# The first layer's first RMS norm takes the route of the other norms, and a subtraction for the rank-64 decay and rate weights changes engine and place

## Chip, core and metric

The kernel runs on one core of one Trainium2 chip. The metric is the device time of a launch in microseconds (us). The kernel before took 1690.54 us as the median of 3 runs (1690.29 to 1692.25).

## What is computed

A decoder trunk of two pre-norm residual layers over 512 positions of width 1024, in float32. What matters here is the head of each layer: an RMS norm, and one wide projection whose columns are then split among three token mixers and their gates.

```python
def rmsnorm(x, g):
    xf = x.astype(jnp.float32)
    y = xf * lax.rsqrt(jnp.mean(xf * xf, axis=-1, keepdims=True) + EPS) * g.astype(jnp.float32)
    return y.astype(x.dtype)
...
    for l in range(DEPTH):
        h = rmsnorm(x, norm1_g[l])
        p = h @ w_in[l]
        p_rw, p_ret, p_sg, gate_logits = jnp.split(p, in_cuts, axis=-1)
        y_rw = rwkv7_branch(p_rw, ...)
...
    # in rwkv7_branch, with wd, ad of rank 64 cut from p
    w = -jax.nn.softplus(-(w0 + jnp.tanh(wd) @ w_up)) - 0.5
    a = jax.nn.sigmoid(a0 + ad @ a_up)
```

## The kernel before, in words

**Layout and precision.** Activations lie with features on the 128 partitions and the 512 positions along the free axis, so that x is eight tiles of 128x512. Products are made to nearly full precision from pairs: each operand is split into a high part (a cast to the fp32r type, on ScalarE, ACT in the profile) and a low part (source minus high, on VectorE, DVE), and `mm3` issues three matmuls for each product (high weight with low x, high with high, low with high). All 128x512 matmuls at line 157 are these.

**The norm is applied late.** The matmuls run on g times x, without the root of the mean square. A finished column group (128 output features, 512 positions, one accumulator bank in PSUM, tile `acc`) is multiplied on its way out of PSUM by `rsF`, a 128x512 tile that holds 1/rms of each position on all partitions (`col`, line 525, output `rwp`). So the matmuls need not wait for the norm, but the first evacuation of an accumulator does. There are four accumulators (pool `pa`) and four smaller result banks (pool `ps`, tile `sm`). A fifth column can start only when one of the first four has been read.

**Layer 0's start.** `run` loads the eight x tiles and the first weight blocks by an order that is written out as a string of steps: z (scale and split of an x tile), s (its square, added up in `acc` of the norm's state, here called the sum of squares, tile `sq`), w (cast and subtraction of one weight block). `firstK` (line 306) then walks the contraction in eight blocks k = 0 to 7 of 128 features, each feeding all four accumulators (columns 12, 4, 0, 8 of the projection; 12 holds the decay and rate ranks): 12 matmuls for each k. Between k = 5 and k = 6 `norm_stats` (line 268) sums the squares over the partitions by four fp32 matmuls with one column (line 272), adds epsilon on VectorE (line 274) and takes the power -1/2 on GpSimd (POOL, line 276). Between k = 6 and k = 7 `norm_rows` (line 279) spreads the result over the partitions by four fp32 transposes (line 281), and ScalarE copies it to `rsF` (line 283).

**The other norms** use `norm_bcast` (line 285): the sum of squares is split into a pair, two fp32r matmuls with a matrix of ones sum and spread it in one go (lines 290 and 291, result `sm`), ScalarE takes the square root (line 293, tile `rms`; it needs another activation table than the one in use), VectorE takes four reciprocals of 128x128 into `rsF` (line 297). In layer 1's first norm a 32x32 block transpose on VectorE (line 300) and four GpSimd copies also make `rsT`, the same numbers with positions on the partitions.

**The rank-64 weights.** `rwkv` loads two 128x512 matrices `wua`, whose two halves of the partitions both hold the same 64 rows; ScalarE casts the whole to fp32r (`wus`, line 515), and GpSimd replaces the lower half by the remainder (line 519), so that one matmul sums both parts. They are used in `prep` (lines 565 and 566).

**Order and queues.** Each engine works through its own list in order. Where a call is wrapped in `keep_in_program_order`, its place among such calls is fixed; all else is placed by a list scheduler of the framework, which sets the order of each engine's list at build time. Weight blocks come by the SyncE DMA queue (SP) into three raw buffers (`wr`), are cast into one of three `wh` buffers and subtracted into one of three `wl` buffers; a load waits until its raw buffer has been cast and subtracted, and a cast waits until TensorE (PE) has used the `wh` buffer's last contents.

Of the kernel before, what the change touches and what calls it, by code (L numbers as in the profile page):

```python
# [16 lines left out]
D = 1024  # L17
S = 512
NC = 4
# [33 lines left out]
class Emit:  # L53
# [91 lines left out]
    def split(self, src, al=None):  # L145

        al = al or self.u
        hi, lo = al(dt=F32R, n="hi"), al(dt=F32R, n="lo")
        self.nc.scalar.copy(hi, src)
        self.nc.vector.tensor_tensor(lo, src, hi, op=SUB)  # L150
        return hi, lo

    def mm3(self, ps, w, x, start, stop, **kw):
# [111 lines left out]
    def norm_new(self):  # L265
        return {"z": [], "acc": None}

    def norm_stats(self, st):
        nc = self.nc
        pt = self.sm((128, 4))  # L270
        for c in range(NC):
            self.tc.keep_in_program_order(nc.tensor.matmul(pt[:, c:c + 1], st["acc"][:, c * 128:c * 128 + 128], self.c("ones")[:, 0:1], start=True, stop=True))
        ms = self.small((128, 4), "ms")
        nc.vector.tensor_scalar(ms, pt, 1.0 / D, 1e-6, op0=MUL, op1=ADD)
        self.rsT = self.small((128, 4), "rs")
        nc.gpsimd.tensor_tensor(self.rsT, ms, self.c("mhalf")[:, 0:4], op=POW)

    def norm_rows(self):
        pb = self.sm()
        for c in range(NC):  # L280
            self.tc.keep_in_program_order(self.nc.tensor.transpose(pb[:, c * 128:c * 128 + 128], self.rsT[:, c:c + 1].to_broadcast([128, 128]), self.c("ident")))
        self.rsF = self.small((128, 512), "rsF", bufs=1)
        self.nc.scalar.copy(self.rsF, pb)

    def norm_bcast(self, st, cols):

        nc, po = self.nc, self.tc.keep_in_program_order
        hi, lo = st["sq"]
        pb = self.sm()
        po(nc.tensor.matmul(pb, self.ones, lo, start=True, stop=False))  # L290
        po(nc.tensor.matmul(pb, self.ones, hi, start=False, stop=True))
        rms = self.u(n="rms")
        nc.scalar.activation(rms, pb, AF.Sqrt, scale=1.0 / D, bias=self.c("eps"))
        self.rsF = self.small((128, 512), "rsF", bufs=1)
        for c in range(NC):
            cs = slice(c * 128, c * 128 + 128)
            nc.vector.reciprocal(self.rsF[:, cs], rms[:, cs])
        if cols:
            t = self.u((128, 4, 4, 32), n="rst")
            nc.vector.transpose(t.rearrange("p c b r -> p (c b r)"), self.rsF)  # L300
            self.rsT = self.small((128, 4), "rs")
            for b in range(4):
                nc.gpsimd.tensor_copy(self.rsT[32 * b:32 * b + 32, :], t[32 * b:32 * b + 32, :, b, 0])

    def firstK(self, st):

        self.h, self.pin = st["z"], True
        pss = [self.acc() for _ in FIRST]
        for k in range(8):
            if k == 6:  # L310
                self.norm_stats(st)
            elif k == 7:
                self.norm_rows()
            hi, lo = self.unit("wk0", 0, k, 0)
            cs = [slice(i * 128, i * 128 + 128) for i in range(NC)]
            if k == 0:
                for w, x in ((hi, 0), (hi, 1), (lo, 0)):
                    for ps, s in zip(pss, cs):
                        self.tc.keep_in_program_order(self.nc.tensor.matmul(ps, w[:, s], self.h[0][x], start=w is hi and x == 0, stop=False))  # L319
                continue  # L320
            for ps, s in zip(pss, cs):
                self.mm3(ps, (hi[:, s], lo[:, s]), self.h[k], False, k == 7)
        self.pin = False
        return pss

    def firstF(self, l, ids, st, at):


        self.h = st["z"]
        pss = [self.acc() for _ in ids]  # L330
        gs = [self.matFg(ps, ("wall", l, i, 0), self.h) for ps, i in zip(pss, ids)]
        self.pin = True
        for i, g in enumerate(gs + gs):
            if i == at:
                self.norm_bcast(st, l and ids[0] == 12)
            next(g)
        self.pin = False
        return pss
# [10 lines left out]
    def run(self):  # L349
        nc, tc, a, V = self.nc, self.tc, self.a, self.nc.vector  # L350
        self.con = self.cp.tile([128, NCC], F32, name="con")
        self.pre, self.tsum = [], {}
        self.rst = self.cp.tile([128, 512], F32, name="rst")
        self.bonesR = self.cp.tile([128, 128], F32R, name="bonesR")
        self.ones = self.cp.tile([128, 128], F32R, name="ones")
        V.memset(self.rst, 1.0)
        wu = self.acc()
        for i in range(5):
            nc.tensor.matmul(wu[:, 0:256], self.rst[:, 0:128], self.rst[:, 256:512], start=True, stop=True)  # L359
        st = self.norm_new()  # L360
        first = tc.tile_pool(name="x0", bufs=1)
        x0 = first.__enter__().tile([128, 520], F32, name="x0g", tag="x0g")
        self.pc = x0[:, 512:520]
        xs = [x0[:, 0:512]] + [self.u(n="x") for _ in range(7)]
        self.keep = True
        with tc.high_priority():
            for j in range(8):
                q, o, i = (nc.scalar, xs[j], a["xT"][:, j, :]) if j in (1, 3) else (nc.sync, xs[j], a["xT"][:, j, :])
                tc.keep_in_program_order(q.dma_start(*((o, i) if j else (x0, a["x0g"]))))
                if self.plan and j in (0, 1, 2):  # L370
                    self.load(self.plan[self.nraw], nc.sync if j else nc.scalar)
        tc.keep_in_program_order(nc.scalar.copy(self.small((128, 1), "ms"), self.rst[:, 0:1]))
        tc.keep_in_program_order(nc.scalar.copy(self.ones, self.rst[:, 0:128]))
        for step in "z0 w z1 w z2 w z3 s0 s1 w z4 s2 z5 s3 w c z6 s4 w z7 s5 s6 s7 w w".split():
            if step == "w":
                if self.plan:
                    if self.nraw == self.npart:
                        self.load(self.plan[self.nraw])
                    self.part(self.plan[self.npart])
            elif step == "c":  # L380
                g1 = self.pc
                self.load_pc(0)
                tc.keep_in_program_order(nc.scalar.dma_start(self.con, a["con"]))
                self.pc, g1 = g1, self.pc
            elif step[0] == "z":
                self.norm_z(st, xs[int(step[1])], "n1")
            else:
                self.norm_sq(st, xs[int(step[1])])
        self.keep, self.pc = False, g1
        first.__exit__(None, None, None)  # L390
        xd = [a["xT"][:, j, :] for j in range(8)]
        for l in range(L):
            mg = self.mixer(l, st)
            st = self.norm_new()
            x = self.wout(l, mg, xd, st)
            st["sq"] = self.split(st["acc"])
            act = self.ffn_up(l, st, x if l == L - 1 else None)
            if l == L - 1:
                self.last(act)
            else:  # L400
                st = self.norm_new()
                x, xd = self.ffn_down(l, act, x, st)
                st["sq"] = self.split(st["acc"])
            self.rp.__exit__(None, None, None)
            self.fp = None
# [88 lines left out]
    def rwkv(self, l, nst):  # L494
# [16 lines left out]
        Ws = []  # L511
        for i in range(2):
            wua, s = self.u(n="wua"), self.u(dt=F32R, n="wus")
            self.tc.keep_in_program_order(nc.scalar.dma_start(wua, a["wua"][l, i]))
            A.copy(s, wua)
            Ws.append((wua, s))
        ready = dict(zip(FIRST, self.firstF(l, FIRST[:3], nst, 3) if l else self.firstK(nst)))
        for i, (wua, s) in enumerate(Ws):
            self.tc.keep_in_program_order(P.tensor_tensor(s[64:128, :], wua[64:128, :], s[64:128, :], op=SUB))
            Ws[i] = s  # L520

        def col(m):
            ps = ready.pop(m) if m in ready else self.colF(l, m)
            p = self.r(n="rwp")
            V.tensor_tensor(p, ps, self.rsF, op=MUL)  # L525
            t = self.r(n="rwc")
            A.activation(t, p, AF.Identity, scale=omu[:, m:m + 1])
            V.scalar_tensor_tensor(t[:, 1:], p[:, :511], self.p("mu", m), t[:, 1:], op0=MUL, op1=ADD)
            return t

        wa = col(12)
        Xs = []
        for i in range(2):
            x = self.u(n="wax")
# [947 lines left out]
```

## Time and profile before

| what | us |
|---|---|
| three runs, median | 1690.54 |
| three runs, lowest and highest | 1690.29 and 1692.25 |
| span of the profiled execution, first to last instruction | 1688.8 |
| TensorE busy in it | 1680.2 |
| VectorE busy | 1217.9 |
| ScalarE busy | 793.7 |
| GpSimd busy | 261.3 |

The profile gives one execution on the chip by its instructions; its own time is its span and the start and end around it, which no row shows. The median of the runs lies 1.74 us above the span, and this difference is taken for what lies around it. A row of the timeline gives start, duration, engine, line, operation, output<-inputs and, in brackets, how long the engine had been idle and what ended that. PE rows are matmuls, whose ends are modelled; the distance between the starts of two matmuls tells more than the duration of one. "x4" means that several instructions were merged in a row.

### The profile page before, as it was taken

To read this page: it belongs to the slowest core of one execution; us is meant where nothing else is said; L and a number is where in the kernel's file an instruction comes from. 1 tells how busy PE (TensorE), PEld (TensorE's weight loads), DVE (VectorE), ACT (ScalarE), POOL (GpSimd) and SP (SyncE) were. 2 spreads that over 40 slices of the span, in tenths; PEclk is the share of its full clock that TensorE was granted. 3 is DMA by queue.
4 is the path that set the end of the run, shared out by engine and by line. 5 is a ranking of instruction groups with operands and counts; after the bars stand their busy time and mean duration, and the time that the engine had idled before them with its cause. 6 is when DMAs were issued, how large, how long until landed. Compare 5 with 4: busy or idle time off the path is not lost.

```text
span 1688.8 us, 27952 instructions
## 1 busy us (share of the span) xinstructions
PE 1680.2 (99%) x10247; PEld 1381.5 (82%) x10247; DVE 1217.9 (72%) x2115; ACT 793.7 (47%) x1365; POOL 261.3 (15%) x376
## 2 busy tenths in 40 slices
PE   9999999999999999999999999999999999999998
PEld 7888877888888888888888888778888888888887
DVE  7887746578669877655568888465786688887877
ACT  6563433554255444433346544335542544444565
POOL 1121000312301200003321210003122012220000
PEclk9999999999999999999999999999999999999999
DMA  5236563634544533247743366536344434443775
GB/s 183 88 109 199 176 187 95 184 122 134 191 144 148 195 122 97 63 146 261 252 145 99 94 207 184 174 101 188 118 137 163 154 96 144 142 141 110 244 248 177
DMA packets 143385, 260.01 MB, mean 154 GB/s; under 512 B 19440, under 2 KB 35440, under 8 KB 143248
## 3 DMA queue, kind: packets, MB, share of 16 engines
q1 hardware_dynamic: 117056, 188.41, 35.9%
q0 software_dynamic: 17552, 54.15, 9.8%
q10 hardware_dynamic: 8640, 15.67, 2.6%
q8 instruction: 80, 1.31, 0.3%
q14 instruction: 57, 0.47, 0.1%
HBM read 212.94 MB, written 45.22 MB: 153 GB/s over the span
## 4 chain that ended last, share of the span: by engine, by line
PE 97%; DVE 1%; DMA 1%; issue 0%; ACT 0%; SPq 0%; ACTq 0%; DVEq 0%
PE acc L157 88%; PE sm L157 3%; PE sm L696 2%; PE sm L948 1%; PE sm L603 1%; PE sm L1059 0%; DMA wr<-wall 0%; DMA tr<-bkT 0%; DVE wl L141 0%; PE acc L359 0%; PE sm L566 0%; PE sm L565 0%; PE sm L1006 0%; PE sm L850 0%; PE acc L319 0%
## 5 line engine op out<-in xcount | busy, mean ns | idle before, releaser
L157 PE MATMUL acc<-lo,sh 128*128 128x512 f32 x1108 | 432.0, 390 | 0.0
L157 PE MATMUL acc<-hi,sh 128*128 128x512 f32 x1108 | 431.4, 389 | 0.0
L157 PE MATMUL acc<-hi,sl 128*128 128x512 f32 x1108 | 424.6, 389 | 0.0
L140 ACT CAST sh<-wr 128x512 fp32r<-128x512 f32 (+1 forms) x375 | 226.8, 614 | 309.1 <-PE acc L157 165.6
L141 DVE TENSOR_TENSOR sl<-wr,sh 128x512 fp32r<-128x512 f32 (+1 forms) x375 | 252.0, 680 | 94.9 <-ACT sh L140 78.9
L141 DVE TENSOR_TENSOR wl<-wr,wh 128x512 fp32r<-128x512 f32 x238 | 169.0, 713 | 139.4 <-ACT wh L140 133.6
L140 ACT CAST wh<-wr 128x512 fp32r<-128x512 f32 x238 | 146.8, 619 | 242.8 <-PE acc L157 154.6
L157 PEld LDWEIGHTS acc<-lo,sh 128*128 128x128 f32 x1108 | 208.0, 188 | 43.8 <-issue 0.3
L157 PEld LDWEIGHTS acc<-hi,sl 128*128 128x128 f32 x1108 | 208.0, 188 | 43.1 <-issue 0.2
L157 PEld LDWEIGHTS acc<-hi,sh 128*128 128x128 f32 x1108 | 208.0, 188 | 43.0
L157 PE MATMUL acc<-lo,wh 128*128 128x512 f32 x584 | 230.0, 394 | 0.4 <-DVE rwp L525 0.4
L157 PE MATMUL acc<-hi,wl 128*128 128x512 f32 x584 | 228.3, 391 | 0.1
L157 PE MATMUL acc<-hi,wh 128*128 128x512 f32 x584 | 227.6, 390 | 0.0
L1125 ACT ACTIVATE cv<-fu,pc 128x512 f32<-128x512 f32 x88 | 71.7, 816 | 138.4 <-DVE fu L1123 138.4
L157 PEld LDWEIGHTS acc<-hi,wl 128*128 128x128 f32 x584 | 109.6, 188 | 24.6 <-issue 0.9
L157 PEld LDWEIGHTS acc<-lo,wh 128*128 128x128 f32 x584 | 109.6, 188 | 24.2 <-DVE rwp L525 0.8
L157 PEld LDWEIGHTS acc<-hi,wh 128*128 128x128 f32 x584 | 109.7, 188 | 22.3 <-issue 0.2
L157 PE MATMUL acc<-ah,sh 128*128 128x512 f32 x352 | 108.4, 389 | 0.0
L1126 DVE SCALAR_TENSOR_TENSOR cv<-fu,pc,cv 128x511 f32<-128x511 f32 x88 | 65.8, 749 | 34.5 <-ACT cv L1125 34.4
L157 PE MATMUL acc<-wl,hi 128*128 128x512 f32 x212 | 85.7, 404 | 0.0
L1123 DVE TENSOR_TENSOR fu<-acc,rsF 128x512 f32<-128x512 f32 x88 | 60.3, 685 | 30.8 <-PE acc L157 29.8
L157 PE MATMUL acc<-wh,hi 128*128 128x512 f32 x212 | 82.5, 389 | 0.0
(368 smaller groups left out, 2447.5 us busy)
## 6 DMA issues: line engine op xcount, KB each, us to landing
wr<-wall SPq DMA_DIRECT2D x480, 256.0 KB, 2.9
gd<-gth ACTq DMA_DIRECT2D x48, 256.0 KB, 3.4
gth<-gd POOLq DMA_DIRECT2D x48, 256.0 KB, 3.7
pre<-wdt POOLq DMA_DIRECT2D x44, 256.0 KB, 6.1
ts<-pre POOLq DMA_DIRECT2D x44, 256.0 KB, 2.8
wr<-ts SPq DMA_DIRECT2D x44, 256.0 KB, 4.1
wr<-wdn SPq DMA_DIRECT2D x40, 256.0 KB, 4.3
wr<-wdt SPq DMA_DIRECT2D x33, 256.0 KB, 4.1
```

Source lines behind the costliest of these rows:

```text
L140: self.kept(self.nc.scalar.copy(hi[:, :n], raw[:, :n]))
L141: self.kept(self.nc.vector.tensor_tensor(lo[:, :n], raw[:, :n], hi[:, :n], op=SUB))
L157: i = self.nc.tensor.matmul(*x, **y, **kw)
L603: i = T.matmul(pK[hv[1 - h], j, :], bk[hv[h], c, 1, :], x[hv[h], c, :], start=True, stop=True)
L696: po(T.matmul(o, l, r, start=start, stop=True, skip_group_check=True))
L948: po(T.matmul(o, lhsT, rhs, start=start, stop=stop, skip_group_check=True))
L1123: V.tensor_tensor(u, ps, self.rsF, op=MUL)
L1125: A.activation(t, u, AF.Identity, scale=self.p("cw2", j), bias=self.p("cb", j))
L1126: V.scalar_tensor_tensor(t[:, 1:], u[:, :511], self.p("cw1", j), t[:, 1:], op0=MUL, op1=ADD)
```

## The change

The first norm's statistics go through `norm_bcast` as well. `norm_stats` and `norm_rows` are gone. The sum of squares is split into a pair at the end of the written-out order of steps (new step "a"), and the two matmuls with ones stand between k = 6 and k = 7. The block transpose and the GpSimd copies become a function `norm_cols`, which `rwkv` calls in both layers behind the first evacuated column. The cast of `wua` and the subtraction, now on VectorE instead of GpSimd, also stand behind that column, in both layers.

```diff
     def split(self, src, al=None):
...
-        self.nc.scalar.copy(hi, src)
-        self.nc.vector.tensor_tensor(lo, src, hi, op=SUB)
+        self.kept(self.nc.scalar.copy(hi, src))
+        self.kept(self.nc.vector.tensor_tensor(lo, src, hi, op=SUB))
...
-    def norm_stats(self, st):
...
-    def norm_rows(self):
...
-    def norm_bcast(self, st, cols):
+    def norm_bcast(self, st):
...
-        if cols:
-            t = self.u((128, 4, 4, 32), n="rst")
...
+    def norm_cols(self):
+
+        nc, t = self.nc, self.u((128, 4, 4, 32), n="rst")
+        nc.vector.transpose(t.rearrange("p c b r -> p (c b r)"), self.rsF)
+        self.rsT = self.small((128, 4), "rs")
+        for b in range(4):
+            nc.gpsimd.tensor_copy(self.rsT[32 * b:32 * b + 32, :], t[32 * b:32 * b + 32, :, b, 0])
 
     def firstK(self, st):
...
-            if k == 6:
-                self.norm_stats(st)
-            elif k == 7:
-                self.norm_rows()
+            if k == 7:
+                self.norm_bcast(st)
...
-        for step in "z0 w z1 w z2 w z3 s0 s1 w z4 s2 z5 s3 w c z6 s4 w z7 s5 s6 s7 w w".split():
+        for step in "z0 w z1 w z2 w z3 s0 s1 w z4 s2 z5 s3 w c z6 s4 w z7 s5 s6 s7 w a w".split():
...
+            elif step == "a":
+                st["sq"] = self.split(st["acc"])
...
             self.tc.keep_in_program_order(nc.scalar.dma_start(wua, a["wua"][l, i]))
-            A.copy(s, wua)
             Ws.append((wua, s))
         ready = dict(zip(FIRST, self.firstF(l, FIRST[:3], nst, 3) if l else self.firstK(nst)))
-        for i, (wua, s) in enumerate(Ws):
-            self.tc.keep_in_program_order(P.tensor_tensor(s[64:128, :], wua[64:128, :], s[64:128, :], op=SUB))
-            Ws[i] = s
...
         wa = col(12)
+        self.norm_cols()
+        for i, (wua, s) in enumerate(Ws):
+            A.copy(s, wua)
+            self.tc.keep_in_program_order(V.tensor_tensor(s[64:128, :], wua[64:128, :], s[64:128, :], op=SUB))
+            Ws[i] = s
```

The scheduler's order changes with it. On TensorE, at the border of k = 6 and k = 7 of layer 0, there stood this before (acc_242 to acc_245 are the four accumulators, wh_213 the weight block of k = 7):

```order
L157 MATMUL acc_245<-hi_179,wl_208 128x512
L281 MATMUL sm_349<-con,rs_325 128x128 x4
L157 MATMUL acc_242<-lo_193,wh_213 128x512
L157 MATMUL acc_242<-hi_192,wh_213 128x512
L157 MATMUL acc_242<-hi_192,wl_214 128x512
```

and now, where the accumulators are acc_244 to acc_247 and the weight block of k = 7 is wh_217:

```order
L157 MATMUL acc_247<-hi_179,wl_208 128x512
L273 MATMUL sm_342<-lo_212,ones 128x512
L274 MATMUL sm_342<-hi_211,ones 128x512
L157 MATMUL acc_244<-lo_193,wh_217 128x512
L157 MATMUL acc_244<-hi_192,wh_217 128x512
L157 MATMUL acc_244<-hi_192,wl_218 128x512
```

The two products with ones take the place of the four transposes; the four one-column matmuls ahead of k = 6 are gone. Behind k = 7 the fifth column follows in both.

On ScalarE, from the cast of k = 7's weights on, before (wh_333, wh_358 and wh_420 are the next three weight blocks, all of columns behind the first four):

```order
L140 CAST wh_213<-wr_211 128x512
L514 DMA wua_234<-wua 128x512
L515 CAST wus_235<-wua_234 128x512
L514 DMA wua_238<-wua 128x512
L140 CAST wh_333<-wr_327 128x512
L515 CAST wus_239<-wua_238 128x512
L140 CAST wh_358<-wr_329 128x512
L283 COPY rsF_354<-sm_349 128x512
L527 ACTIVATE rwc_378<-rwp_376,omu_221 128x512
```

and now, with wh_217 for k = 7 and wh_326, wh_354 and wh_425 for the next three blocks:

```order
L149 CAST hi_211<-sq_202 128x512
L140 CAST wh_217<-wr_215 128x512
L499 DMA wua_238<-wua 128x512
L499 DMA wua_241<-wua 128x512
L140 CAST wh_326<-wr_320 128x512
L140 CAST wh_354<-wr_322 128x512
L276 ACT_TABLE_LOAD
L276 ACTIVATE rms_345<-sm_342,con 128x512
L140 CAST wh_425<-wr_324 128x512
L515 CAST wus_239<-wua_238 128x512
L515 CAST wus_242<-wua_241 128x512
L508 ACTIVATE rwc_372<-rwp_370,omu_225 128x512
```

A table load and the root stand where the copy of `rsF` stood, behind the cast of the second of the next blocks; the casts of `wus` moved behind them.

On VectorE, before the first evacuation of an accumulator (`rwp`), before:

```order
L141 TENSOR_TENSOR wl_334<-wr_327,wh_333 128x512
L274 TENSOR_SCALAR ms_323<-sm_318 128x4
L141 TENSOR_TENSOR wl_359<-wr_329,wh_358 128x512
L525 TENSOR_TENSOR rwp_376<-acc_242,rsF_354 128x512
L525 TENSOR_TENSOR rwp_402<-acc_243,rsF_354 128x512
```

and now:

```order
L141 TENSOR_TENSOR wl_327<-wr_320,wh_326 128x512
L141 TENSOR_TENSOR wl_355<-wr_322,wh_354 128x512
L280 RECIPROCAL rsF_347<-rms_345 128x128 x4
L141 TENSOR_TENSOR wl_426<-wr_324,wh_425 128x512
L506 TENSOR_TENSOR rwp_370<-acc_244,rsF_347 128x512
L285 STREAM_TRANSPOSE rst_375<-rsF_347 128x512
L516 TENSOR_TENSOR wus_239<-wua_238,wus_239 64x512
L506 TENSOR_TENSOR rwp_407<-acc_245,rsF_347 128x512
L516 TENSOR_TENSOR wus_242<-wua_241,wus_242 64x512
```

Four reciprocals and the subtraction for a third block now stand ahead of the first `rwp`, and the transpose and the two subtractions for `wus` ahead of the second and the third.

Further down on VectorE, where the operand `bk` of layer 0's first group of 64x128 matmuls is finished, there stood before (acc_673 is the ninth column):

```order
L528 SCALAR_TENSOR_TENSOR rwc_670<-rwp_668,pc_176,rwc_670 128x511
L141 TENSOR_TENSOR wl_695<-wr_650,wh_694 128x512
L594 TENSOR_TENSOR rwc_404<-rwc_404,cs_565 128x512
L141 TENSOR_TENSOR sl_737<-wr_692,sh_736 128x512
L525 TENSOR_TENSOR rwp_710<-acc_673,rsF_354 128x512
L595 TENSOR_TENSOR bk_563<-rwc_404,cs_565 128x8x64
```

and now (acc_636 is the eighth column):

```order
L141 TENSOR_TENSOR wl_658<-wr_537,wh_657 128x512
L580 TENSOR_TENSOR rwc_409<-rwc_409,cs_570 128x512
L506 TENSOR_TENSOR rwp_673<-acc_636,rsF_347 128x512
L141 TENSOR_TENSOR wl_682<-wr_637,wh_681 128x512
L581 TENSOR_TENSOR bk_568<-rwc_409,cs_570 128x8x64
```

`bk` moved one column forward. Otherwise, the order of layer 0's recurrence preparation differs in many places without a change of its work: among others, the first pair of matmuls for `bonus` (tile `bonesR`, lines 620 and 621 of before) stood 4 accumulator matmuls behind the first group of 64x128 matmuls and now stands 49 behind it, and that group (output `sm`, inputs X and bk) stands 23 matmuls earlier. In layer 1 the order of TensorE differs by six matmuls at one place.

More of the change, by code (lines that the diff above doesn't have):

```diff
@@ L266, in norm_new @@
         return {"z": [], "acc": None}
-    def norm_stats(self, st):
[L269 to L276, printed above, removed]
-    def norm_rows(self):
[L279 to L283, printed above, removed]
-    def norm_bcast(self, st, cols):
+    def norm_bcast(self, st):
         nc, po = self.nc, self.tc.keep_in_program_order
@@ L297, in norm_bcast @@
             nc.vector.reciprocal(self.rsF[:, cs], rms[:, cs])
-        if cols:
-            t = self.u((128, 4, 4, 32), n="rst")
[L300 to L303, printed above, removed]
+    def norm_cols(self):
[4 more added lines that the diff above has]
+            nc.gpsimd.tensor_copy(self.rsT[32 * b:32 * b + 32, :], t[32 * b:32 * b + 32, :, b, 0])
     def firstK(self, st):
@@ L334, in firstF @@
             if i == at:
-                self.norm_bcast(st, l and ids[0] == 12)
+                self.norm_bcast(st)
             next(g)
```

## The prediction

> **What bounds the kernel now.** I read the page first: the span, TensorE's busy time and the shares by engine of the chain that ended last.
>
> ```profile
> span 1688.8 us, 27952 instructions
> PE 1680.2 (99%) x10247; PEld 1381.5 (82%) x10247; DVE 1217.9 (72%) x2115; ACT 793.7 (47%) x1365; POOL 261.3 (15%) x376
> PE 97%; DVE 1%; DMA 1%; issue 0%; ACT 0%; SPq 0%; ACTq 0%; DVEq 0%
> ```
>
> TensorE is the bound nearly throughout. An edit off TensorE costs nothing unless it makes TensorE wait, and an edit on TensorE counts in full. The waits of TensorE, longest first:
>
> ```profile
> PE acc L359 <- DVE rst L356: 1.5, 1, 1.5
> PE sm L620 <- ACT Y L608: 0.5, 1, 0.5
> PE sm L696 <- DVE s L756: 0.4, 2, 0.2
> PE acc L157 <- DVE rwp L525: 0.4, 1, 0.4
> ```
>
> There is next to nothing left to win from waits: the last row is the one that the changed norm ends, the second is in layer 0's preparation of the recurrence. So the question is narrow: what TensorE saves at the first norm, and how long it will wait there. The timeline of TensorE at that place:
>
> ```profile
> 21.65 0.39 PE L157 MATMUL acc<-hi,wl 128*128 128x512 f32 x1
> 21.88 0.94 PE L272 MATMUL sm<-con,sq 128*128 128x1 f32 x8
> 22.69 0.49 PE L157 MATMUL acc<-lo,wh 128*128 128x512 f32 x1
> 23.01 0.40 PE L157 MATMUL acc<-hi,wh 128*128 128x512 f32 x1
> ...
> 25.33 0.39 PE L157 MATMUL acc<-hi,wl 128*128 128x512 f32 x1
> 25.73 0.65 PE L281 MATMUL sm<-con,rs 128*128 128x128 f32 x4
> 26.14 0.48 PE L157 MATMUL acc<-lo,wh 128*128 128x512 f32 x1
> 26.45 0.39 PE L157 MATMUL acc<-hi,wh 128*128 128x512 f32 x1
> ...
> 28.75 0.39 PE L157 MATMUL acc<-hi,wl 128*128 128x512 f32 x1
> 29.50 0.50 PE L157 MATMUL acc<-lo,wh 128*128 128x512 f32 x1 [0.36 <-DVE rwp L525]
> ```
>
> A 128x512 matmul is followed by the next after 0.23 us. The row at 28.75 is the last matmul of k = 7; the one at 29.50 opens the fifth column, which needs the accumulator that the first `rwp` frees. I call this start T0. It is 29.50 now, 0.52 us later than 28.75 + 0.23. Behind T0 TensorE has the same matmuls before and after, so the change is worth the shift of T0 plus what later waits gain or lose.
>
> **What it removes and adds on TensorE.** The one-column matmuls take 22.69 - 21.88 = 0.81 us, and the first step behind them is 23.01 - 22.69 = 0.32 instead of 0.23: 0.90 in all. The transposes cost 26.14 - (25.33 + 0.23) = 0.58, and 0.08 in the step behind: 0.66. The two products with ones are seen in layer 1's second norm, with the root that reads them:
>
> ```profile
> 1350.25 0.39 PE L291 MATMUL sm<-hi,ones 128*128 128x512 f32 x1
> 1350.48 0.39 PE L157 MATMUL acc<-lo,sh 128*128 128x512 f32 x1
> ...
> 1350.68 0.69 ACT L293 ACTIVATE rms<-sm,con 128x512 f32<-128x512 f32 x1 [2.69 <-PE sm L291]
> ```
>
> Each fills one ordinary step of 0.23. So 0.46 is added and 1.56 removed: TensorE is ready for the fifth column 1.10 us earlier, at 28.75 + 0.23 - 1.10 = 27.88. The same rows give the delay from a matmul's start to a waiting ScalarE instruction: 1350.68 - 1350.25 = 0.43.
>
> **The new chain that ends in the first `rwp`.** The sum of squares is there in time, so the matmuls with ones do not wait:
>
> ```profile
> 19.02 2.28 DVE L231 TENSOR_TENSOR sq<-sq,sq 128x512 f32<-128x512 f32 x3
> ...
> 28.77 1.27 DVE L525 TENSOR_TENSOR rwp<-acc,rsF 128x512 f32<-128x512 f32 x2
> ```
>
> It ends at 21.30; a cast and a subtraction (0.62 and 0.63, as the next rows have such work) give the pair by 22.7, and the products stand at 21.88 + 12 x 0.23 = 24.6. The rest of the chain is the one of layer 1's first norm, in the timeline of ScalarE and VectorE:
>
> ```profile
> 861.97 0.62 ACT L515 CAST wus<-wua 128x512 fp32r<-128x512 f32 x1 [0.34 <-DMA wua<-wua]
> 862.61 1.28 ACT L293 ACT_TABLE_LOAD   x1
> 863.91 0.69 ACT L293 ACTIVATE rms<-sm,con 128x512 f32<-128x512 f32 x1
> ...
> 864.63 3.39 DVE L297 RECIPROCAL rsF<-rms 128x128 f32<-128x128 f32 x4 [2.27 <-ACT rms L293]
> 867.93 0.63 DVE L141 TENSOR_TENSOR wl<-wr,wh 128x512 fp32r<-128x512 f32 x1
> 868.48 0.70 DVE L300 STREAM_TRANSPOSE rst<-rsF 128x512 f32<-128x512 f32 x1
> 869.10 0.65 DVE L525 TENSOR_TENSOR rwp<-acc,rsF 128x512 f32<-128x512 f32 x1
> ```
>
> In the new order of ScalarE the table load stands directly behind the cast of the second weight block of the columns to come (wh_354), and on VectorE one more weight subtraction stands between the reciprocals and `rwp`. From that cast's start: 0.64 to the load (862.61 - 861.97), 1.30 to the root, 0.72 to the reciprocals, 3.30 to the subtraction, 0.55 to `rwp`, 0.67 for it, 0.06 to TensorE (28.77 + 0.67 = 29.44 against 29.50): 7.24 us. There layer 1 hides all this, since half a block of three columns and a free accumulator lie behind its products; in layer 0 only k = 7 does, 12 matmuls or 2.7 us.
>
> When does that cast start? It needs its raw block, whose load in the present trace leaves at 21.9, and the `wh` buffer of k = 6. The tile's view for 21 to 30 us:
>
> ```profile
> L127 SPq DMA_DIRECT2D wr<-wall x4: 327/328/1539, 21.9 to 28.9; - x4
> DMA to landing us min/median/max: 2.6/3.2/4.3
> ```
>
> k = 6 gives its buffer back at 21.88 + 11 x 0.23 + 0.43 = 24.8. The load lands at 21.9 + 3.2 = 25.1 by the median (24.5 to 26.2 by the ends). ScalarE's queue now issues both loads of `wua` close behind its start, where one of them came before; so I take 25.3. T0 is then 25.3 + 7.24 = 32.5, **3.0 us later than now**. By the ends: 24.8 gives 32.0 (+2.5), 26.2 gives 33.4 (+3.9). So TensorE, ready at 27.88, waits 4.7 us where it waited 0.5. Queued behind the reciprocals on VectorE are the subtraction, `rwp`, the transpose and the other `rwp`s; the second `rwp` is needed one column (5.4 us) after the first, so only the first one holds TensorE.
>
> **What else moves, and what hides it.** The subtractions for `wus` leave GpSimd and cost VectorE a step of 0.60 each (1.27 - 0.67 in the row of two), with the transpose's 0.62 (869.10 - 868.48): 1.8 us behind the first `rwp`; the table load back to tanh is another 1.3 on ScalarE. The stretches behind (30 to 60, then 60 to 95 us) have room for this; their rows give the length and then the busy time of PE, PEld, DVE, ACT and POOL:
>
> ```profile
> 30.00:60.00 30.00, 30.00 (x133) 24.80 (x133) 25.68 (x42) 20.78 (x36) 4.52 (x4) 1.00 0.41 123
> 60.00:95.00 35.00, 34.55 (x261) 28.01 (x260) 27.21 (x44) 20.35 (x35) 9.30 (x8) 1.00 0.20 61
> ```
>
> VectorE is idle for 4.3 and 7.8 us there, and TensorE itself is 3.0 us later. The nearest consumer at risk is the first group of 64x128 matmuls, which moved 23 matmuls forward: it would start at T0 + 132 x 0.227 = 62.5. `bk` now follows the eighth column, the fourth from T0 with four matmuls for decay and rate among them (100 x 0.227 = 22.7): read at T0 + 23.1, then `wl` and `bk`, ready near 57.6. A cover of 4.9 us, the earlier group included. The transposed columns (GpSimd copies) and layer 1's same move lie off TensorE's path: layer 1's TensorE shows no wait there, and its GpSimd list only gets shorter. I put all these at nothing. If VectorE's cover failed, each us late would be a us of time.
>
> One wait should go. The rows of TensorE behind the first group:
>
> ```profile
> 67.58 0.40 PE L157 MATMUL acc<-hi,wh 128*128 128x512 f32 x1
> 68.43 0.50 PE L620 MATMUL sm<-lo,bonesR 128*128 128x512 f32 x1 [0.45 <-ACT Y L608]
> ```
>
> 68.43 - 67.58 - 0.23 = 0.62 us, spent on a result bank that ScalarE still copies. In the new order 49 matmuls (11 us) instead of 4 stand ahead of this product, so the bank is free: -0.6, between -0.6 and nothing if another wait takes its place.
>
> **The sum:** +3.0 - 0.6 = **+2.4 us**. On the profiled execution 1688.8 becomes 1691.2; with the 1.74 us that lie between the span and the median, 1692.9. That is 0.14%, and about 0.2% (3.4 us) is what a measurement of this kernel can tell from no change.
>
> **The rivals.**
>
> *A late weight block ahead of the root.* The table load stands behind a cast that waits for a DMA; the slowest load in that window took 4.3 us. With 26.2 as the landing T0 moves by 3.9, and if the bank wait of 0.6 stays in another form nothing comes off: 1690.5 + 3.9 = 1694.4, slower. It decides from a landing at 25.7, 0.4 later than I take, if no wait goes, or from 26.3 if it does. For it: three loads in a burst; against it: the median.
>
> *A dearer table switch.* In the rows above the root starts 1.30 us behind the load's start, so the switch costs the load alone. If the engine had to empty around the switch for as long again as the load takes (1.28), T0 would be 33.8 and the time 1694.2, slower; against it, the rows of layer 1 show nothing between the cast's end at 862.59 and the load, nor between the load's end at 863.89 and the root. The Trainium skill, page "ScalarE: Activation LUTs", section "What ACT_TABLE_LOAD costs", gives about 1283 ns for the load and about 1380 ns for a drain, 2.66 us for each switch; by it the time would be 1694.3, an estimate. The trace agrees with its first figure and not with its second.
>
> *VectorE falls behind* in layer 0's preparation and TensorE waits for `bk` or for weight lows: over 1 us beyond the 4.9 of cover is needed, 1694 and more.
>
> *The norm stays covered*, because the load lands early and the scheduler's order does not hold TensorE: then only TensorE's savings count, -1.1 - 0.5 - 0.6 = -2.2, 1688.3. Against it stand 4.7 us of chain beyond k = 7.
>
> **How the numbers follow.** My forecast (+2.4) has 0.64; the late block 0.15; the dearer switch 0.05; VectorE's backlog 0.07; the covered norm 0.04; 0.05 is left for a gain over 3.4 that I see no row for. Slower by over 0.2% are the second to fourth: 0.27; within 0.2%: 0.68; faster: 0.05. The range: the early end of the load gives +2.5 - 0.6 = +1.9, and a second wait of the size of 0.6 may go in the stretch that follows, with half a us for the scatter of the runs: +0.5, 1691.0. The late end with no wait gone gives +3.9, and the same half us: +4.4, 1694.9. Outside lie the covered norm, the unseen gain and the larger part of VectorE's backlog.
>
> **What would show it.** Right: no row for 128x1 matmuls; TensorE at 24.6 in the two products; a wait of TensorE of about 4.5 us for the first `rwp`, T0 near 32.5; the root right behind the table load near 27.2, reciprocals near 27.9; no wait at the first `bonesR` product; beyond 100 us every stage later by the same 2 to 3 us. Wrong: T0 below 31 or above 34, a new wait of over 1 us behind T0, or a layer 1 that differs in length.

## The result, and the profile after

| runs | us, median | lowest to highest |
|---|---|---|
| before, 5 runs on the same chip | 1690.32 | 1690.28 to 1692.25 |
| after, 5 runs | 1700.37 | 1700.06 to 1703.62 |

The ratio is 1.0062, with a 95% interval of 1.005 to 1.0074. The change makes the kernel 10 us slower. The forecast was 1692.9, and its range ended at 1694.9: the loss is four times the 2.4 us that I had worked out. The profiled execution after took 1700.3 us, and its span is 1698.59, 9.74 longer than before (1688.85).

The page of the kernel after: the span, the busy time, and the shares of the chain that ended last.

```profile
span 1698.6 us, 27937 instructions
PE 1682.7 (99%) x10237; PEld 1383.5 (81%) x10237; DVE 1221.1 (72%) x2124; ACT 796.5 (47%) x1368; POOL 251.9 (15%) x375
PE 88%; issue 4%; DMA 3%; DVE 3%; ACT 1%; POOL 0%; SPq 0%; ACTq 0%; DVEq 0%; POOLq 0%
```

Two things stand out. TensorE has ten instructions fewer, but its busy time is 2.5 us longer: something makes matmuls slower. And the chain, which was 97% TensorE, now leaves TensorE for 12% of the span. The waits of TensorE, longest first (total, times, longest):

```profile
PE acc L157 <- DVE rwp L506: 6.1, 1, 6.1
PE acc L342 <- DVE rst L339: 1.5, 1, 1.5
PE acc L157 <- DVE wl L141: 1.1, 2, 0.6
PE acc L157 <- ACT wh L140: 0.5, 1, 0.5
...
PE sm L682 <- DVE S L731: 0.4, 1, 0.4
```

The first row is the forecast wait, 6.1 us where I had 4.7. The third, fourth and last rows are new. The wait for `Y` at the first `bonesR` product is gone. The timeline of TensorE at the border of k = 7 and the fifth column, and that of ScalarE and VectorE in the chain that it waits for:

```profile
24.85 0.39 PE L273 MATMUL sm<-lo,ones 128*128 128x512 f32 x1
25.07 0.39 PE L274 MATMUL sm<-hi,ones 128*128 128x512 f32 x1
...
27.79 0.39 PE L157 MATMUL acc<-hi,wl 128*128 128x512 f32 x1
34.23 0.77 PE L157 MATMUL acc<-lo,wh 128*128 128x512 f32 x1 [6.05 <-DVE rwp L506]
34.79 0.63 PE L157 MATMUL acc<-hi,wh 128*128 128x512 f32 x1
35.22 0.63 PE L157 MATMUL acc<-hi,wl 128*128 128x512 f32 x1
```

```profile
21.27 0.82 ACTq L499 DMA_DIRECT2D wua<-wua  x2
21.70 1.14 ACT L140 CAST wh<-wr 128x512 fp32r<-128x512 f32 x2
26.91 0.62 ACT L140 CAST wh<-wr 128x512 fp32r<-128x512 f32 x1 [4.06 <-DMA wr<-wall]
27.55 1.28 ACT L276 ACT_TABLE_LOAD   x1
28.84 0.69 ACT L276 ACTIVATE rms<-sm,con 128x512 f32<-128x512 f32 x1
```

```profile
29.56 3.39 DVE L280 RECIPROCAL rsF<-rms 128x128 f32<-128x128 f32 x4 [1.31 <-ACT rms L276]
32.86 0.63 DVE L141 TENSOR_TENSOR wl<-wr,wh 128x512 fp32r<-128x512 f32 x1
33.41 0.68 DVE L506 TENSOR_TENSOR rwp<-acc,rsF 128x512 f32<-128x512 f32 x1
```

The chain itself is as forecast: from the cast at 26.91 to T0 at 34.23 it takes 7.32 us, against 7.24. The cast is late, since its weight block is: ScalarE was idle for 4.06 us until the load landed. The rows of TensorE behind T0 hold the second cost: the steps between matmuls are 35.22 - 34.79 = 0.43 us instead of 0.23. Three windows of TensorE: start and end, length, busy time, matmuls in brackets, the granted clock (1.00 is full speed), and the share and GB/s of the DMA:

```profile
29.50:32.91 3.41, 0.00 (x0) 1.00 0.18 62
32.91:36.32 3.41, 2.09 (x5) 0.50 0.23 77
36.32:39.74 3.42, 3.42 (x9) 0.50 0.00 0
```

The clock fell while TensorE waited, at 32.91, and stayed halved until 39.74 us. Against the same dense matmuls of before, counted by their starts, the 9.74 us come from these places:

| stretch | later by, us |
|---|---|
| start to the first product's first matmul (5.59 against 5.35) | 0.25 |
| to T0 (34.23 against 29.50) | 4.48 |
| the first 24 matmuls behind T0: 8.12 us against 5.57 | 2.55 |
| the next 360, with the `bonesR` wait that is gone | -0.73 |
| the next 420 (138 to 248 us): three waits for weights | 2.38 |
| the rest of layer 0 | 0 |
| layer 1: one wait at 1109 us | 0.7 |
| the rest, in steps under 0.1 | 0.1 |

The first product starts between 5.2 and 5.6 us in the twelve traces of this study, so I take the first row for scatter; no kernel was traced twice. The weight waits end at 163, 167 and 201 us. The view counts 1.6 us of idle time for them; by the starts of the matmuls they and the slower step behind each cost the 2.38. SyncE's queue shows why they come. First after, then before, at the first round trip of `bkT`:

```profile
153.90 0.44 SPq L243 DMA_DIRECT2D tr<-bkT  x1
158.34 0.77 SPq L639 DMA_DIRECT2D bkS<-tr  x2
159.21 0.37 SPq L127 DMA_DIRECT2D wr<-wall  x1
```

```profile
141.17 0.43 SPq L243 DMA_DIRECT2D tr<-bkT  x1
141.69 0.38 SPq L127 DMA_DIRECT2D wr<-wall  x1
145.90 1.73 SPq L653 DMA_DIRECT2D bkS<-tr  x4
```

`bkT` takes a round trip through memory: it is written to `tr` and read back as `bkS`, and the reads must wait until the write has landed (153.90 to 158.34). Before, a weight load follows the write at once (141.69), and the reads come behind it. After, two of the reads stand ahead of the next weight load, and it waits with them.

### The profile page after: what moved, and what is told of

It reads as the page before. It is cut to its first block, busy times and chain, and to the rows that moved or that the text cites. A ratio compares the mean times of both kernels' runs of the same rounds, so it can differ in the third digit from the quotient of the medians.

```text
span 1698.6 us, 27937 instructions
## 1 busy us (share of the span) xinstructions
PE 1682.7 (99%) x10237; PEld 1383.5 (81%) x10237; DVE 1221.1 (72%) x2124; ACT 796.5 (47%) x1368; POOL 251.9 (15%) x375
## 4 chain that ended last, share of the span: by engine, by line
PE 88%; issue 4%; DMA 3%; DVE 3%; ACT 1%; POOL 0%; SPq 0%; ACTq 0%; DVEq 0%; POOLq 0%
PE acc L157 80%; PE sm L157 3%; PE sm L682 2%; DMA wr<-wall 1%; PE sm L934 1%; PE sm L589 1%; DVE wl L141 1%; DMA tr<-yt 1%; PE sm L1045 0%; DMA tr<-bkT 0%; ACT wh L140 0%; DMA wr<-wk 0%; DMA x<-xT 0%; DVE TMP L806 0%; DVE cs L808 0%
## 5 line engine op out<-in xcount | busy, mean ns | idle before, releaser
L157 PE MATMUL acc<-wh,lo 128*128 128x512 f32 x212 | 82.5, 389 | 0.0
```

Of the source, the lines that this page charges most:

```text
L157: i = self.nc.tensor.matmul(*x, **y, **kw)
```

## The experiments

I had two theories when I began. A: the norm's new route costs the time, by the late chain and by what TensorE's idle time does to its clock. B: the moved subtractions on VectorE cost it. Later runs took apart the three costs that the trace shows: the late T0, the halved clock, and the waits for weights. The kernel before was timed beside each group of experiments: 1690.84 (the first four), 1690.49 (the next four), 1690.85 (the last two). Its executions beside one group spread over 3.5 us (1689.39 to 1692.89), so where a kernel ran once its trace tells more than its total.

**The norm alone.** The subtractions for `wus` go back to GpSimd, and its casts ahead of the products.

```diff
             self.tc.keep_in_program_order(nc.scalar.dma_start(wua, a["wua"][l, i]))
+            A.copy(s, wua)
...
+        for i, (wua, s) in enumerate(Ws):
+            self.tc.keep_in_program_order(P.tensor_tensor(s[64:128, :], wua[64:128, :], s[64:128, :], op=SUB))
+            Ws[i] = s
...
-        for i, (wua, s) in enumerate(Ws):
-            A.copy(s, wua)
-            self.tc.keep_in_program_order(V.tensor_tensor(s[64:128, :], wua[64:128, :], s[64:128, :], op=SUB))
-            Ws[i] = s
```

> First part of the change alone: the norm by products with ones, but the casts of wua ahead of the first columns and their subtraction on GpSimd, as before. Theory A (a late cast ahead of the table load delays the root, and the long idle time then halves TensorE's clock): the table load now also stands behind the cast of the second wua, whose load leaves only when the first has been cast (near 24) and lands near 27; cast 27.0, load 27.7, T0 near 34.3, half clock for about 5 us after it, so 1696 to 1698 without the later weight waits and up to 1700 with them. Theory B (the work moved to VectorE is what costs): VectorE is relieved of the two subtractions, T0 at 32.5 or less, no more than 1693.

Measured: 1701.21 us (one run). T0 is 34.83.

```profile
PE acc L157 <- DVE rwp L510: 6.6, 1, 6.6
...
PE acc L157 <- DVE wl L141: 1.2, 2, 0.7
PE acc L157 <- ACT wh L140: 1.0, 1, 1.0
```

All three costs are there without the second part: the wait at T0, the clock (half from 32.91 for 6.83 us) and the weight waits. Theory A holds; B falls for these.

**The subtractions for `wus` alone**, with the norm as before (edited from the changed kernel).

```diff
+    def norm_stats(self, st):
...
+    def norm_rows(self):
...
-            if k == 7:
-                self.norm_bcast(st)
+            if k == 6:
+                self.norm_stats(st)
+            elif k == 7:
+                self.norm_rows()
```

> Second part alone: the norm as in the kernel before, the casts of wua and the subtraction (now VectorE's) behind the first column. Theory A: the norm's chain is short, T0 stays at 29 to 30 although both loads of wua now run ahead of a weight block, TensorE never idles long, full clock throughout; 1689.5 to 1691.5, no change. Theory B: VectorE, with 1.2 us more behind the first evacuation, makes TensorE wait for weight lows or bk: slower by 3 us and more, 1693.5 or above.

Measured: 1692.44 us, 10 runs, ratio 1.0012 (1.0002 to 1.0021). T0 is 29.29, and TensorE does not wait there at all. The new waits in its trace are two for weights, ending at 158.6 and 192.4 us:

```profile
PE acc L157 <- DVE wl L141: 0.8, 2, 0.5
```

This trace is of the shortest of the ten runs, 1690.83 us, no longer than the kernel before. So it shows a cost of the second part in these waits, and not where all of the median's 1.6 us lie.

**The loads of `wua` later.** In layer 0 they are issued behind the first evacuated column, so that they do not share the DMA with the weight block.

```diff
-            self.tc.keep_in_program_order(nc.scalar.dma_start(wua, a["wua"][l, i]))
+            if l:
+                self.tc.keep_in_program_order(nc.scalar.dma_start(wua, a["wua"][l, i]))
...
-            A.activation(t, p, AF.Identity, scale=omu[:, m:m + 1])
+            i = A.activation(t, p, AF.Identity, scale=omu[:, m:m + 1])
+            if m == 12 and l == 0:
+                self.tc.keep_in_program_order(i)
+                for j, (wua, _) in enumerate(Ws):
+                    self.tc.keep_in_program_order(nc.scalar.dma_start(wua, a["wua"][l, j]))
```

> The changed kernel with layer 0's two loads of wua issued only behind the first column's evacuation. Theory A: the weight block ahead of the table load no longer shares the DMA engines with them and lands near 24.6 instead of 26.8; its cast starts at 24.8 when k = 6 gives the buffer back; T0 near 32.0 instead of 34.2, idle time of about 4.2 us instead of 6.2. If the clock needs more idle time than that to fall, 1692.5 to 1695; if not, 2.5 us more. Rival (the landing is late by itself, whatever else is loaded): T0 stays at 34 and the time at 1700.

Measured: 1695.51 us (one run). ScalarE's rows, where the cast and the table load come 1.34 us earlier than in the changed kernel:

```profile
25.57 0.62 ACT L140 CAST wh<-wr 128x512 fp32r<-128x512 f32 x1 [2.47 <-PE sm L273]
26.21 1.28 ACT L276 ACT_TABLE_LOAD   x1
```

T0 is 32.90, near the 32.5 of the prediction and 0.9 later than expected for this run: the load landed at 25.47, not near 24.6. (The first row names a product with ones as the releaser, but that matmul starts only at 25.19. The landing is 0.10 ahead of the cast, as in the changed kernel with 26.81 and 26.91.) TensorE still waits 4.4 us, and the clock is halved for one stretch, 3.41 us: the 24 matmuls behind T0 take 7.17 us. SyncE's order is that of before, and no weight waits are left between 150 and 210 us.

**Sixteen useless matmuls behind k = 7**, into a result bank that nothing reads, to keep TensorE at work in the wait.

```diff
+        pd = self.sm()
+        for _ in range(16):
+            self.tc.keep_in_program_order(self.nc.tensor.matmul(pd, self.ones, self.h[7][0], start=True, stop=True))
```

> The changed kernel with 16 more 128x512 matmuls of ones with a part of x between k = 7 and the fifth column, into a bank that nobody reads (work without use: 3.6 us of TensorE). Theory A (idle time halves the clock): T0 stays at 34.2, since the chain through ScalarE and VectorE sets it, the idle time shrinks from 6.2 to 2.6 us, the steps behind T0 are 0.23 and not 0.43, and the time falls by about 2.5 us to 1698 although TensorE does more. Rival (the clock falls for another reason at this place, such as the load on the chip): steps of 0.43 stay, 1700 or more.

Measured: 1695.86 us (one run). TensorE does 3.6 us more work and the kernel is 4.5 us faster than the changed one. T0 is 34.07, 0.2 earlier than there, but the clock stays at 1.00 (windows as above):

```profile
27.50:34.00 6.50, 5.21 (x23) 1.00 0.12 42
34.00:36.00 2.00, 1.93 (x9) 1.00 0.36 131
```

So the idle time is what halves the clock. It is 1.4 us here where 2.6 was expected, in part by luck: the first four matmuls of the first product took 1.97 us in this execution (5.60 to 7.57; 1.12 in the changed kernel), so that the last matmul of k = 7 starts 0.9 us later, while the chain that sets T0 does not. The 4.5 us aren't the clock's alone: the scheduler gave SyncE's queue the order of before in this kernel, and the weight waits went as well (a wait of 1.0 for `U`, ending at 235.5 us, came).

**Eight useless matmuls** instead of sixteen (the same edit with `range(8)`).

> As the run with 16 useless matmuls, with 8: idle time about 3.2 us, between the 1.4 that kept the full clock and the 4.4 (late wua loads) that lost it. It brackets the idle time from which TensorE's clock falls. If it falls: steps of 0.43 for 3 to 7 us behind T0 and about 1697; if not: steps of 0.23 and about 1695.5, as with 16.

Measured: 1698.54 us (one run), 1.5 above the expected figure for a clock that falls. The wait at T0 is 3.4 us, and the clock falls, for one stretch:

```profile
31.56:34.97 3.41, 0.57 (x3) 1.00 0.06 14
34.97:38.38 3.41, 3.41 (x10) 0.50 0.17 63
```

An idle time of 1.4 us keeps the clock, and one of 3.4 loses it. The fall comes 0.57 us after TensorE has resumed work.

**The root first.** With the loads of `wua` late as above, the root and the reciprocals get a fixed place ahead of the second next block's cast and subtraction.

```diff
-        nc.scalar.activation(rms, pb, AF.Sqrt, scale=1.0 / D, bias=self.c("eps"))
+        self.kept(nc.scalar.activation(rms, pb, AF.Sqrt, scale=1.0 / D, bias=self.c("eps")))
...
-            nc.vector.reciprocal(self.rsF[:, cs], rms[:, cs])
+            self.kept(nc.vector.reciprocal(self.rsF[:, cs], rms[:, cs]))
...
+            self.keep = k == 7
             if k == 7:
                 self.norm_bcast(st)
             hi, lo = self.unit("wk0", 0, k, 0)
+            self.keep = False
```

> The kernel with late wua loads, and besides the root and the reciprocals fixed in order ahead of the cast and the subtraction of the second next weight block. Theory A (the table load and the root stand behind a cast that waits for a DMA): the root starts when the products with ones are done, near 25.4, reciprocals near 26.1; with two weight subtractions between them and the first rwp T0 is near 31.1 (33 with late loads alone), idle time 3 us. Its SyncE queue has the same order of loads as the changed kernel's, so the waits for weights between 155 and 205 us, some 2 us, should be back: 1692 to 1695. Rival (the chain is slow whatever stands ahead of the root): T0 stays near 33.

Measured: 1697.11 us (one run), slower than with the late loads alone. The chain did what was expected, as ScalarE's row of the root shows (28.84 in the changed kernel):

```profile
25.29 0.69 ACT L276 ACTIVATE rms<-sm,con 128x512 f32<-128x512 f32 x1 [1.23 <-PE sm L274]
```

T0 is 31.29. But the idle time is still 3.3 us and the clock still falls for 3.41 us (the 24 matmuls take 7.17 us). SyncE's queue is back in the order of the changed kernel with its weight waits (ending at 164 and 198 us), as expected. One more wait, of 0.7, ends at 1596. The expectation of 1692 to 1695 was missed: I had left out the clock, and that a new order can bring a wait elsewhere.

**The first accumulator copied raw.** On top of the root first, ScalarE copies the first accumulator out of its bank without the norm, so that the fifth column need not wait for the norm at all.

```diff
+            if m == 12 and l == 0:
+                raw = self.u(n="raw")
+                self.tc.keep_in_program_order(A.copy(raw, ps))
+                ps = raw
```

> The root-first kernel, in which ScalarE copies layer 0's first finished accumulator out of its bank without the norm, and VectorE multiplies the copy later. Theory A (only the first rwp holds TensorE): the fifth column no longer depends on the norm, T0 is near 28.0, where TensorE is ready, no idle time, full clock; 1.3 us less than before at T0 and the saved bank wait: 1688.5 to 1690.5, some 10 us below the changed kernel and at or under the kernel before, unless the order of SyncE's queue gives up to 2 us back. Theory B (VectorE is the bound there): 1695 and more.

Measured: 1695.78 us, 7 runs, ratio 1.0031 (1.0019 to 1.0042): missed. The wait at T0 is gone (29.02, with TensorE at work up to it), but the new order opens another at the first `bonesR` product, long enough to lose the clock again (half from 72.54 for 6.83 us):

```profile
69.53 0.40 PE L157 MATMUL acc<-hi,wh 128*128 128x512 f32 x1
73.81 0.80 PE L617 MATMUL sm<-lo,bonesR 128*128 128x512 f32 x1 [3.88 <-ACT Y L605]
```

This trace is of the longest of the seven runs, 1699.70 us; the other six lie between 1695.06 and 1696.52, so some 4 us of it are not in the median. That the clock fell in all seven is likely: their mean granted clock is 0.997 or 0.998, as in the changed kernel, against 0.999 and 1.0 in the kernel before.

**The round trips of `bk` on another queue.** The changed kernel, with layer 0's writes of `bkT` and the reads behind them issued by GpSimd, so that SyncE's queue holds no part of these trips there.

```diff
-            d = self.trip(t, nc.sync)
+            q = nc.sync if l else nc.gpsimd
+            d = self.trip(t, q)
...
-                turn(o[:, 256 * a:256 * a + 256], d[:, 256 * a:256 * a + 256], lambda h: h ^ a)
+                turn(o[:, 256 * a:256 * a + 256], d[:, 256 * a:256 * a + 256], lambda h: h ^ a, q)
```

> The changed kernel with layer 0's round trips of bk through DRAM on GpSimd's DMA queue instead of SyncE's, so that no weight load stands behind them. Theory A (of the 10 us, some 2 are weight loads that the new order of SyncE's queue puts behind reads of bk, which wait for a write to land): T0 and the half clock stay as in the changed kernel, the waits of TensorE for weights at 162, 166 and 200 us vanish, about 1698. Theory B (VectorE has fallen behind with its additional work): these waits stay, about 1700.

Measured: 1699.44 us (one run). Of the weight waits one of 0.3 us is left, and the 420 matmuls in question take 107.3 us, against 109.4 in the changed kernel and 107.0 before. By 870 us the kernel is 2.7 us ahead of the changed one: 2.1 from these, and 0.8 from the clock, which was halved from 31.53 to 38.36, more of it before T0 (34.54), so that the 24 matmuls behind T0 take 7.31 us instead of 8.12, less 0.3 for the later T0. But the time fell by 0.9 only, since layer 1 became 1.8 us longer, 0.7 of it by the wait for `S`, which grew to 1.1:

```profile
PE sm L683 <- DVE S L732: 1.1, 1, 1.1
```

**The same for the second part alone**: the subtractions for `wus` as changed, the norm as before, the round trips by GpSimd. It adds the last diff to the second kernel of this section.

> Only the second part of the change (the subtractions for the rank-64 weights on VectorE behind the first evacuated column), with the round trips of bk in layer 0 issued by GpSimd's queue. Theory A (what the second part costs, about 1 us above the end of the fourth column, comes only from weight loads that stand behind the reads of bk in SyncE's queue): no wait of TensorE for wl at 158 and 191 us, the fifth column starts at 29.3, and the time is 1690 to 1691, the same as before. Rival B (VectorE is too full for the moved subtractions, wherever the loads stand): the waits stay and the time is 1692.4 again.

Measured: 1689.86 us, 11 runs, ratio 0.9995 (0.9985 to 1.0004). All the waits of TensorE that the view lists:

```profile
PE acc L359 <- DVE rst L356: 1.5, 1, 1.5
PE sm L697 <- DVE s L757: 0.4, 2, 0.2
```

T0 is 29.20 and no weight wait is left. Theory A of this run holds, for the waits: they go with the round trips, while VectorE keeps the moved work. The 420 matmuls take 106.4 us, against 108.1 with the round trips on SyncE's queue. As a whole the kernel is no different from before. The kernel before with its round trips moved wasn't run, so what that move is worth by itself is open.

**Late loads and sixteen useless matmuls**, the two edits above together.

> The changed kernel with layer 0's loads of wua issued behind the first evacuated column, and 16 useless matmuls with ones (3.6 us) behind k = 7. Theory A (three separate costs: the late start of the fifth column, the clock that falls, the weight loads): the fifth column starts at 32.9, TensorE idles for 0.8 us, the clock stays full, no waits for weights between 150 and 210 us, and the time is the 1695.5 of the late loads less 1.6 for the clock, 1693.9, or 3.4 above before. Rival B (the 1.6 is not the clock's, it lies in the order behind): 1695.5 again.

Measured: 1697.37 us, 5 runs, ratio 1.0036 (1.0023 to 1.005): missed. The clock stayed at 1.00, and the 24 matmuls behind T0 take 5.52 us, 1.65 less than with the halved clock, as A had it. T0 was even earlier than expected, at 32.25. But the order of the program is another one again, with its own waits:

```profile
PE sm L614 <- ACT GB L601: 1.4, 1, 1.4
PE sm L690 <- ACT U L727: 0.9, 1, 0.9
```

So the clock's 1.6 us is right for its place, and the sum isn't: the costs can't be added up across kernels whose order differs.

No version that has the new norm came within the time of before.

## Why the prediction was wrong, step by step

- **TensorE's savings: right.** The last matmul of k = 7 starts at 27.79, which puts TensorE ready at 28.02, with a start that is 0.25 late in this execution; I had 27.88. The two products fill ordinary steps (24.85 to 25.30).
- **The chain of 7.24 us: right** (7.32). The table load costs 1.28 and the root follows at 1.29, so the dearer table switch didn't come.
- **"So I take 25.3" for the start of the cast: wrong, a term of the sum that was too small.** Measured are 26.91, or 26.66 without the late start. The load left at 21.77 and landed at 26.81, 5.03 us later, behind both loads of `wua` at 21.27 and 21.64. I had added 0.2 us for those loads, and my upper bound came from the slowest load in a trace with one of them. The rival of the late weight block was the right mechanism, with a bound that was still too low. With the loads moved away the same load takes 3.84 us, and T0 is 32.9. This is 1.4 us of the miss.
- **"TensorE, ready at 27.88, waits 4.7 us", and then counted only as a shift of T0: the step that failed most.** I wrote that "behind T0 TensorE has the same matmuls before and after", and so it has, but not at the same speed: after an idle time of over 3 us the clock is halved for 3.41 or 6.83 us. That costs 2.55 us in the changed kernel and 1.6 with the late loads; no term and no rival had it. Even on my own numbers, 4.7 us of idle time, it would have been due: 3.3 us were enough in the root-first kernel.
- **"I put all these at nothing" for what else moves: wrong by 3.1 us.** I looked for cover on VectorE and on GpSimd, and VectorE did have it: the second part with the round trips moved keeps the work on VectorE, and no weight wait is left. What I passed over is the list of SyncE's queue, where weight loads came to stand behind reads that wait for a round trip. The weight waits (2.4 us) go when the round trips leave that queue. The 0.7 in layer 1 I can't assign: waits for `S` of 0.4 to 1.1 us appear there in three of the kernels and not in the others, and no run tells why.
- **The bank wait at `bonesR`: right.** It is gone, and the stretch is 0.73 us shorter.

With these sizes the forecast of 2.4 becomes 2.4 + 1.4 for the load + 2.55 for the clock + 2.4 + 0.7 for the waits + 0.25 for the start = 9.7, against 9.74. Of the signs of being wrong that I had named, T0 above 34 and a layer 1 of another length came; the clock was in none of them.

## What to carry to other kernels

A wait of TensorE of some 3 us and more costs more than its length: look for the row of the granted clock behind it, and price the halved stretch as a term of its own. When a load decides the path, count every transfer that is issued in the microsecond ahead of it on any queue. And when a scheduler redoes the order, compare the DMA queues' lists too: a load behind a read that waits for a round trip is a new wait, though its engine has idle time.

## What the runs showed of the hardware

**When the clock falls.** Each halved stretch that lies within the work lasts 3.41 or 6.83 us. The windows of 3.41 us ahead of its start and behind it, in the kernel with the root first and in the one with the round trips on GpSimd's queue:

```profile
28.72:32.13 3.41, 0.84 (x4) 1.00 0.35 102
32.13:35.54 3.41, 3.41 (x10) 0.50 0.71 208
```

```profile
28.12:31.53 3.41, 1.05 (x5) 1.00 0.22 79
31.53:34.94 3.41, 0.40 (x1) 0.50 0.03 7
34.94:38.36 3.42, 3.42 (x9) 0.50 0.21 70
```

A window with 1.05 us of work or less led to the half clock; a fully busy one brought full clock back; one with 2.09 at half clock, in the changed kernel above, did not. At full clock a window with 2.04 us of work kept it (31.35 to 34.76 with sixteen useless matmuls). The full clock ahead of the first fall also lasts a whole number of 3.41 us: 8 of them from 5.61 to 32.91 in the changed kernel, 7 from 7.63 to 31.53 with the round trips moved. All this fits a check at the end of fixed windows of 3.41 us; the rule was not tried by itself, and how much work keeps the clock, between 1.05 and 2.04 us, is open. The Trainium skill, page "TensorE: Matmul & The Clock Gate", section "What's actually happening", describes free-running windows of 3413 ns and a clock of 4/8 after an idle one. The trace agrees with the length and the half, and shows that a window need not be wholly idle.

**How loads share.** The load of 256 KB that the chain waits for leaves SyncE's queue between 21.6 and 22.3 us. With both `wua` loads within 0.6 us ahead of it, it took 4.86 to 5.16 us to land (four kernels); with one, 4.49 (the norm alone); with none, 3.77 to 3.84 (three kernels) and 2.56 (late loads and sixteen matmuls). Why this last one was faster is open.
